# The feed-forward by seven block products for eight, in a fused Conformer and RG-LRU layer on one core

## The chip, the core and the metric

The kernel runs on one core of a Trainium2 chip. A core has five engines that the texts below name: TensorE (PE; PEld is its loading of weights) multiplies matrices, VectorE (DVE) and ScalarE (ACT) work element by element on 128 partitions, GpSimd (POOL) does smaller work of that kind and can start transfers, and SyncE (SP) only starts transfers between the chip's memory and the core's own memory, SBUF. TensorE writes its results into PSUM, from where VectorE or ScalarE must take them. Each engine works through its own instructions in the order of the program and waits at semaphores for the others. The metric is the device time of one execution in microseconds (us).

## What is computed

One inference step of one layer, on 544 tokens (512 of a prompt and 8 x 4 of samples), model width 1024, all in float32. Ahead of the part that matters here come two token mixers, their merge, and a first normalisation; the result is x1. Then:

```
x1  = layer_norm(alpha * x + mix)
hid = square(relu(x1 @ w_ff1))            # w_ff1 1024 x 4096
ff  = hid @ w_ff2                         # w_ff2 4096 x 1024
ple = sigmoid(x1 @ w_ple_gate) * (p @ w_ple_proj)
y   = layer_norm(alpha * x1 + ff + ple)
```

## The kernel before

All activations lie feature by feature: a tile holds 128 channels (partitions) by 544 tokens. float32 products are made in three passes of a shorter format: each operand is split into a high part (`hi`, by ScalarE) and a low part (`lo` = value minus high part, by VectorE), and a product is high x high + high x low + low x high. So each block of 128 x 128 weights against 544 tokens takes three passes, each in two halves of 288 and 256 columns, since a bank of PSUM holds 512.

**Weights** come as chunks of 512 x 256 (128 x 1024 in SBUF, 512 KB), 64 of them for the feed-forward, in the order of use. SyncE loads a chunk into one of `RAW_BUFS = 3` raw buffers, ScalarE makes `hi`, VectorE `lo`, into four buffers each (`SPLIT_BUFS`), and TensorE uses it in `pair`: two column tiles of the output, a PSUM tile `ps` of 1024 columns (two banks; three such buffers, ring `mm`) for each. A second ring `misc` has two PSUM buffers of one bank.

**Feed-forward.** `ff_order` interleaves the four quarters of the first matrix (`evac_ff1`: relu and square by ScalarE from PSUM, then the split) with the four of the second (`evac_ff2`: VectorE adds the PSUM tile to the running sum `acc`). The last quarter is done by token halves (`by_halves`, PSUM tile `psq`), so that the last normalisation (`between3`) starts beside it. The feed-forward has 64 x 48 = 3072 matmuls.

**The order of the program** is written by a planner while the kernel is built. `Clocks` keeps an estimate of when each engine is free and each tile ready. `stream` offers the next load (SP), high part (ACT) or low part (DVE) of the weights, `put` queues sequences of steps beside the products, and `fill`, called after each few matmuls, puts into each engine's queue what its estimated clock allows; `need` forces what is due. What comes out is a fixed order on each engine. Dependencies between engines follow from it: an instruction that writes a tile waits for the earlier readers of that tile, one that reads waits for its writer, by semaphore.

`SLOTS` is the number of activation tiles in SBUF. All instructions of the kernel are recorded by one helper, at line 137 in the program before and line 149 after, so the profile's groups are told apart by the tiles' names.

Of the kernel before, what the change touches and what calls it, by code (L numbers as in the profile page):

```python
# [9 lines left out]
F32 = mybir.dt.float32  # L10
# [5 lines left out]
P = 128  # L16
# [7 lines left out]
# the 544 token columns lie in two PSUM banks, as 256 + 288 neighbouring columns  # L24
# [3 lines left out]
SLOTS = 71  # L28
# [12 lines left out]
LN1_PRIO = 0.1  # L41
STREAM_PRIO = 0.15
# [19 lines left out]

def tname(x):
    return x.tensor.name
# [9 lines left out]
class Clocks:  # L74
    """estimates of when each engine comes to its work, from which the order of issue follows"""
# [35 lines left out]
    def op(self, e, name, out, args, kw):  # L111
# [4 lines left out]
        if e == "D":  # L116
# [25 lines left out]
def tile_hybrid_step(ctx: ExitStack, tc: tile.TileContext, I, O):  # L142
# [35 lines left out]
    # ---------------------------------------------------------------- constants  # L178
# [11 lines left out]
    # TensorE has its full clock only after a stretch of work: begin that while the first loads are under way  # L190
# [5 lines left out]
    # ---------------------------------------------------------------- weight stream  # L196
# [15 lines left out]

    raws, his, splits, held, fast, stacked = {}, {}, {}, set(), set(), set()
# [11 lines left out]
    def parts(j, tag):  # L225
        """a chunk's split weights: one buffer, or two of the activations' for a chunk that is held for long"""
# [34 lines left out]
    def split_first(a, b):  # L261
        """columns a to b of the first chunk, which comes in pieces"""
# [16 lines left out]
    def stream(e, i):  # L279
        """the next load, high or low part of a weight that engine e may take up beside chunk i"""  # L280
# [70 lines left out]
    def fill():  # L351
        horizon = clocks.t["T"] + LEAD
        moved = True
        while moved:
            moved = False
            for e in "DSVGT":
                while clocks.t[e] < horizon:
                    now = clocks.t[e]
                    it = stream(e, state["next"] - 1)
# [23 lines left out]
    # ---------------------------------------------------------------- products  # L383
# [13 lines left out]
    def pair(acts, mt0, evac, nkt=None):  # L397
        """two 128-column tiles of a product; its chunks come next in the stream"""
# [13 lines left out]
    def by_halves(acts, mt0, nmt, evac, between=None):  # L412
        """column tiles, all of the first token half before the second"""
# [21 lines left out]
    def split_later(prio, src, name, done_, due, *deps):  # L435
        """the two parts of an activation as a sequence of its own"""
# [18 lines left out]
    # ---------------------------------------------------------------- stream order  # L455
# [32 lines left out]
    ff_order = [(1, 0), (1, 1), (2, 0), (1, 2), (2, 1), (1, 3), (2, 2), (2, 3)]  # L488
    for kind, q in ff_order:
        if kind == 1:  # L490
            plan(I["w_ff1"][0], D, 1024 * q, 4)
        else:
            for p in range(4):
                for r in range(2):
                    w_spec(I["w_ff2"][0], 1024 * q + 512 * r, 4, 256 * p, 256)
    held.update(range(len(specs) - 4, len(specs)))

    # ---------------------------------------------------------------- x, feature-major
# [27 lines left out]
    # ---------------------------------------------------------------- parameters and states  # L526
# [37 lines left out]
    def param_math():  # L564
        # softplus(-lam) = max(-lam, 0) + 2 atanh(e / (2 + e)), e = exp(-|lam|)
# [19 lines left out]
        # c2 * r is half of -log(a)  # L585
# [3 lines left out]
    # ---------------------------------------------------------------- layer norms  # L589
    class Norm:  # L590
        """mean and variance over the 1024 channels of eight feature-major tiles, per token half"""
# [52 lines left out]
        def put(self, h, prio, due, after, *deps):  # L644
            """queue the steps up to 1 / deviation, and then after()"""
# [101 lines left out]
    # ---------------------------------------------------------------- branch b  # L747
# [519 lines left out]
```

## Time and profile before

| | us |
|---|---|
| median of 3 runs (1005.08 to 1007.27) | 1005.63 |
| span of the profiled execution | 1004.8 |
| around the span, against the median of the runs | 0.8 |
| VectorE busy | 646.2 |
| ScalarE busy | 413.1 |
| GpSimd busy | 179.6 |
| TensorE's unbroken last stretch, nearly all of it feed-forward | 604.57 to 972.31 |

The page gives for each engine busy time, its share of the span and the number of instructions. A group of instructions has the line, engine, operation, the tiles written and read (buffer numbers left out) and their shapes, the count, then busy time and mean nanoseconds, then the idle time before them and what ended most of it. A chain row has start, duration and instruction; a timeline row the same, with the idle time before it and what ended that in brackets. A transfer's row ends with the median time from issue to landing. In a row of the windows stand the stretch, its length, each engine's busy time with its count of instructions, the granted clock of TensorE (1.00 is full), the share in which the DMA engines were busy, and GB/s.

### The profile page before, as it was taken

What the parts mean: (1) busy time and instruction counts of PE and PEld (TensorE: products, weight loads), DVE (VectorE), ACT (ScalarE), POOL (GpSimd) and SP (SyncE); (2) the same over time, 40 slices, a digit from 0 to 9 for tenths busy, and PEclk for the clock granted to TensorE, in tenths of its full rate; (3) what the DMA queues carried; (4) which work ended last, traced back from release to release, by engine and by line L of the source; (5) the groups of instructions that cost most, each with busy time, mean ns of one, the idle gap of its engine ahead of it and who ended that gap; (6) DMA issues with size and microseconds to landing.
All of it is one profiled execution on the core that took longest, in us unless ns stands there. A gap on an engine that the chain in (4) does not pass through costs nothing.

```text
span 1004.8 us, 17739 instructions
## 1 busy us (share of the span) xinstructions
PE 964.2 (96%) x7560; PEld 959.4 (95%) x7560; DVE 646.2 (64%) x939; ACT 413.1 (41%) x600; POOL 179.6 (18%) x173
## 2 busy tenths in 40 slices
PE   8999979989889997999999999999999999999995
PEld 8999979989889997999999999999999999999995
DVE  5698889897899999794468952323322222233447
ACT  6432428643467321563225834455114511541301
POOL 0342765455332700001200000000000000000002
PEclk9999989999899998999999999999999999999998
DMA  8333324332332222326251402222232332222402
GB/s 291 93 95 103 107 65 155 104 100 61 88 117 73 64 78 91 107 84 197 84 169 43 125 24 84 85 84 85 87 99 73 97 108 84 85 84 85 125 29 84
DMA packets 89279, 97.87 MB, mean 97 GB/s; under 512 B 4208, under 2 KB 82416, under 8 KB 89200
## 3 DMA queue, kind: packets, MB, share of 16 engines
q1 hardware_dynamic: 89200, 96.74, 31.1%
q8 instruction: 59, 0.97, 0.4%
q14 instruction: 20, 0.16, 0.1%
HBM read 89.71 MB, written 3.81 MB: 93 GB/s over the span
## 4 chain that ended last, share of the span: by engine, by line
PE 72%; DVE 12%; POOL 7%; ACT 5%; issue 3%; DMA 1%; SPq 0%; DVEq 0%; ACTq 0%; POOLq 0%
PE ps L137 55%; PE psq L137 14%; DVE ca L137 5%; DVE lo L137 2%; POOL prod L137 2%; POOL cbs L137 2%; POOL ctx_b L137 1%; PE pps L137 1%; ACT th L137 1%; PE rg L137 1%; ACT L137 1%; ACT hi L137 1%; ACT aa L137 1%; DVE s L137 1%; DVE th L137 1%
## 5 line engine op out<-in xcount | busy, mean ns | idle before, releaser
L137 ACT ACTIVATE hi<-raw 128x1024 fp32r<-128x1024 f32 (+4 forms) x177 | 167.7, 957 | 284.1 <-PE ps L137 217.2
L137 DVE TENSOR_TENSOR lo<-raw,hi 128x1024 fp32r<-128x1024 f32 (+3 forms) x173 | 194.4, 1148 | 13.2 <-ACT hi L137 13.0
L137 DVE SCALAR_TENSOR_TENSOR ca<-u,par_a,ca 128x482 f32<-128x482 f32 (+29 forms) x240 | 179.6, 806 | 1.3 <-ACT ca L137 0.9
L137 PE MATMUL ps<-x1l,hi 128*128 128x288 f32 x616 | 128.3, 290 | 0.6 <-DVE x1l L137 0.6
L137 PE MATMUL ps<-x1h,hi 128*128 128x288 f32 x616 | 127.6, 289 | 0.6 <-ACT x1h L137 0.6
L137 PE MATMUL ps<-x1h,lo 128*128 128x288 f32 x616 | 127.6, 288 | 0.0
L137 PEld LDWEIGHTS ps<-x1h,hi 128*128 128x128 f32 x616 | 94.8, 189 | 0.8 <-ACT x1h L137 0.8
L137 PEld LDWEIGHTS ps<-x1l,hi 128*128 128x128 f32 x616 | 94.6, 189 | 0.8 <-DVE x1l L137 0.8
L137 PEld LDWEIGHTS ps<-x1h,lo 128*128 128x128 f32 x616 | 94.9, 189 | 0.0
L137 POOL TENSOR_TENSOR y<-y,rows_g 128x512 f32<-128x512 f32 x2 | 3.1, 1547 | 461.1 <-ACT y L137 461.1
L137 DVE TENSOR_TENSOR acc<-acc,ps 128x544 f32<-128x544 f32 x24 | 17.3, 722 | 93.8 <-PE ps L137 93.8
L137 ACT ACTIVATE ff<-ps 128x544 f32<-128x544 f32 x32 | 20.0, 624 | 51.2 <-PE ps L137 51.2
L137 POOL TENSOR_TENSOR prod<-ctx_a,par_a 128x248 f32<-128x248 f32 x32 | 36.9, 1206 | 0.0
L137 PE MATMUL psq<-x1l,hi 128*128 128x288 f32 (+1 forms) x128 | 36.9, 288 | 0.0
L137 PE MATMUL psq<-x1h,lo 128*128 128x288 f32 (+1 forms) x128 | 36.8, 288 | 0.0
L137 PE MATMUL psq<-x1h,hi 128*128 128x288 f32 (+1 forms) x128 | 36.8, 287 | 0.0
L137 PE MATMUL ps<-x0h,hi 128*128 128x288 f32 x104 | 23.2, 306 | 10.5 <-ACT gate L137 9.0
L137 PEld LDWEIGHTS ps<-x0h,hi 128*128 128x128 f32 x104 | 16.7, 198 | 11.7 <-ACT gate L137 9.7
L137 PE MATMUL ps<-x0h,lo 128*128 128x288 f32 x104 | 22.3, 297 | 5.3 <-DVE lo L137 5.3
L137 ACT ACT_TABLE_LOAD x20 | 25.7, 1283 | 1.4 <-PEq L1257 0.7
L137 POOL COPY ctx_b<-bx 128x32 f32<-128x32 f32 x10 | 21.2, 2125 | 26.6 <-ACT bx L137 26.6
L137 POOL TENSOR_TENSOR sa<-sa,sb 128x544 f32<-128x544 f32 x6 | 10.9, 1812 | 77.3 <-DVE sa L137 77.3
(616 smaller groups left out, 2647.7 us busy)
## 6 DMA issues: line engine op xcount, KB each, us to landing
raw<-in_w_ff_dram SPq DMA_DIRECT2D x64, 512.0 KB, 4.2
raw<-in_w_in_dram SPq DMA_DIRECT2D x51, 512.0 KB, 3.6
xr<-in_x_dram SPq DMA_DIRECT2D x16, 272.0 KB, 5.3
raw<-in_w_proj_b_dram SPq DMA_DIRECT2D x8, 512.0 KB, 3.4
raw<-in_w_proj_a_dram SPq DMA_DIRECT2D x8, 512.0 KB, 4.1
raw<-in_w_out_dram SPq DMA_DIRECT2D x8, 512.0 KB, 3.5
raw<-in_w_ple_gate_dram SPq DMA_DIRECT2D x8, 512.0 KB, 3.9
out_dram<-y SPq DMA_DIRECT2D x8, 256.0 KB, 2.0
```

Of the source, the lines that this page charges most:

```text
L137: return fn(out, *args, **kw)
```

## The change

The feed-forward's two products are made by a form of Strassen's and Winograd's scheme for 2 x 2 blocks. With weight blocks A11, A12, A21, A22 (128 x 128 each, several such in a row) and activation blocks B (two channel tiles by two halves of 272 tokens), a product of eight block products becomes seven, from sums of blocks:

| number | weights | activations | goes to PSUM region |
|---|---|---|---|
| 1 | A11 | B11 | al |
| 7 | S3 = A11 + A21 | t3 | de |
| 6 | S2 = S3 + A22 | t2 | al, onto 1 |
| 4 | A22 | t4 | de, onto 7 |
| 5 | S1 = A21 + A22 | t1 | al, onto 1 and 6 |
| 2 | A12 | B21 | be |
| 3 | S4 = S2 + A12 | B22 | al, onto all before |

The table is also the order on TensorE. al and be are the two banks of one PSUM tile of the ring `mm`, de is one of the ring `misc`. After each product its region is read: in the first matrix by ScalarE after 1, 7, 6 and 3 and by VectorE after 4, 5 and 2; in the second always by VectorE, which adds it to a block of `acc` or subtracts it.

The first matrix is done in 16 groups `f0` to `f15` of 256 output channels, the second in five stages `g0` to `g4` over 256-channel blocks of hid, each with four groups of output channels. f0 and g4 stay with plain products (`FOUR`), the others use seven (`SEVEN`): 15 groups of products of 128 x 512 weights (256 KB) and 16 of 128 x 384 (192 KB). The order is f0 to f3, g0, f4 to f6, g1, f7 to f9, g2, f10 to f13, g3, f14, f15, g4.

Of the weight sums, S1 and S3 are made in the transfer: SP loads the first block into a raw buffer, then GpSimd starts an accumulating DMA that adds the second. S2 and S4 are added by VectorE from raw buffers. Two products' weights (units) share a buffer of a ring, of which there are still three raw and four of each split part. Each unit is then split as before. VectorE also makes the activations' forms t1 to t4, which ScalarE and VectorE split. The weights are laid out by blocks in memory. Cut to its core:

```diff
-SLOTS = 71
+SLOTS = 72
+FORM_AHEAD = {"D": 7, "G": 6, "V": 4, "S": 5}
+HALF = T // 2
+SUMS_BY_DMA = True
...
+    SEVEN = ("A11", "S3", "S2", "A22", "S1", "A12", "S4")
+    FOUR = ("A11", "A12", "A21", "A22")
...
+                def load(u=u, first=first, nm=nm):
+                    have_raw(u)
+                    DMA.dma_start(u.raw, u.src[first])
+                    u.full = nm[0] == "A"
+                    u.begun = True
+                task("D", u, lambda u=u: may_have("raw", u.r), lambda: 0.0, load)
+                if nm[0] == "S" and by_dma:
+                    def more(u=u, second=PARTS[nm][1]):
+                        G.dma_start(u.raw, u.src[second], accum_op=OP.add)
+                        u.full = True
+                    task("G", u, lambda u=u: u.raw is not None, lambda: 0.0, more)
...
+        elif by_dma:
+            lo(us["A11"])
+            total(us["S2"], us["S3"], us["A22"])
+            lo(us["S3"]), lo(us["S2"])
+            lo(us["A22"]), lo(us["S1"])
+            total(us["S4"], us["S2"], us["A12"])
+            lo(us["A12"]), lo(us["S4"])
...
+    def seven(fs, name, after):
+        ab, d = mm_psum(name), misc_psum(name + "d")
+        al, be, de = ab[:, :HALF], ab[:, 512:512 + HALF], d[:, :HALF]
+        for nm, ps, start, b in ((1, al, True, "B11"), (7, de, True, "t3"), (6, al, False, "t2"), (4, de, False, "t4"),
+                                 (5, al, False, "t1"), (2, be, True, "B21"), (3, al, False, "B22")):
+            u = take()
+            for k, f in enumerate(fs):
+                mm3(ps, u, k, f()[b], start and k == 0, k == len(fs) - 1, not start)
+                fill()
+            release(u)
+            after(nm, ps)
+            fill()
...
+    def ff2_seven(g):
+        q0, nq = GROUPS[g]
+        for mp in range(4):
+            c = [[half(acc[2 * mp + i], l) for l in range(2)] for i in range(2)]
+            def after(nm, ps):
+                out, op = {1: (c[0][0], V.tensor_add), 7: (c[1][1], V.tensor_sub), 6: (c[1][0], V.tensor_sub),
+                           4: (c[1][0], V.tensor_sub), 5: (c[1][1], V.tensor_sub), 2: (c[0][0], V.tensor_add),
+                           3: (c[0][1], V.tensor_add)}[nm]
+                op(out, out, ps)
+            seven([lambda q=q: hid_forms[q] for q in range(q0, q0 + nq)], f"g{g}_{mp}", after)
```

What this does to the order is seen at three places of the second matrix. On VectorE before, in the second matrix, each pair of readings of PSUM (`acc`) stands between low parts of chunks (`lo`) that are whole loads of SP:

```order
L137 TENSOR_TENSOR acc2_6260<-acc2_6260,ps116_0_7944 128x544
L137 TENSOR_TENSOR acc3_6261<-acc3_6261,ps116_1_7945 128x544
L137 TENSOR_TENSOR lo120_8060<-raw120_7892,hi120_8000 128x1024
L137 TENSOR_TENSOR lo121_8114<-raw121_7950,hi121_8058 128x1024
L137 TENSOR_TENSOR acc4_6262<-acc4_6262,ps118_0_8056 128x544
L137 TENSOR_TENSOR acc5_6263<-acc5_6263,ps118_1_8057 128x544
```

On VectorE now, in the third group of the third stage (`g2_2` is its tile with al and be, `g2_2d` the one with de; `fraw70` holds S1 in its second half, `fraw71` S4 in its second, `fraw72` the next group's A11 and S3, `fraw73` its S2):

```order
L149 TENSOR_TENSOR acc5_6263<-acc5_6263,g2_2_9491 128x272
L149 TENSOR_TENSOR flo70_9509<-fraw70_9449,fhi70_9508 128x384
L149 TENSOR_TENSOR fraw71_9468<-fraw69_9428,fraw71_9468 128x384
L149 TENSOR_TENSOR acc5_6263<-acc5_6263,g2_2d_9492 128x272
L149 TENSOR_TENSOR flo71_9539<-fraw71_9468,fhi71_9538 128x384 x2
L149 TENSOR_TENSOR flo72_9561<-fraw72_9542,fhi72_9560 128x384
L149 TENSOR_TENSOR acc5_6263<-acc5_6263,g2_2_9491 128x272
L149 TENSOR_TENSOR fraw73_9550<-fraw72_9542,fraw73_9550 128x384
L149 TENSOR_TENSOR flo72_9561<-fraw72_9542,fhi72_9560 128x384
L149 TENSOR_TENSOR flo73_9587<-fraw73_9550,fhi73_9586 128x384
L149 TENSOR_TENSOR acc4_6262<-acc4_6262,g2_2_9491 128x272
```

The first row reads product 6, the fourth product 4, the seventh product 5 and the last product 2; the sum S2 of the next group (`fraw73`) now stands between the readings of 5 and 2.

On TensorE in the same group, with the semaphores that an instruction waits for (`hh` and `hl` tiles are high and low parts of activation forms):

```order
L149 MATMUL g2_2_9491<-hh8B_9195,fhi70_9508 128x272
L149 MATMUL g2_2_9491<-hl8B_9228,fhi70_9508 128x272
L149 MATMUL g2_2_9491<-hh8B_9195,flo70_9509 128x272
L149 MATMUL g2_2_9491<-hh6A_8437,fhi71_9538 128x272 [waits DVE_49,Activation_49]
L149 MATMUL g2_2_9491<-hl6A_8470,fhi71_9538 128x272
```

The third row ends product 5, and the fourth begins product 2, in the other bank of the same tile; its wait on VectorE is for the reading of product 5, as the first matmul of product 3 waits for that of product 2.

More of the change, by code (lines that the diff above doesn't have):

```diff
@@ L279, in stream @@
     def stream(e, i):
+        if forms is not None and {"D": state["loaded"], "S": state["hi"], "V": state["lo"]}.get(e, INF) >= len(specs):
+            return forms.offer(e)
         more = 2 if i in fast else 0
@@ L487, in tile_hybrid_step @@
     plan(I["w_ple_gate"][0], D, 0, 4)
[L488 to L496, printed above, removed]
     x = []
@@ new lines, in tile_hybrid_step, with offer, run, take @@
+    add_units.r = add_units.s = 0
+    class forms:
+        @staticmethod
+        def offer(e):
+            if not tasks.get(e):
+                return None
+            i, gate, when, fn = tasks[e][0]
+            if i > at["now"] + FORM_AHEAD[e] or not gate():
+                return None
+            def run():
+                tasks[e].popleft()
+                fn()
+            return when(), run
+    def take():
+        at["now"] += 1
+        u = units[at["now"]]
+        need(NCH + u.i)
+        while not getattr(u, "lo_done", False):
+            moved = False
+            for e in "DGSV":
+                while tasks[e] and tasks[e][0][0] <= u.i + 3 and tasks[e][0][1]():
+                    tasks[e].popleft()[3]()
+                    moved = True
+                    if u.lo_done:
+                        break
+            assert moved, (u.i, u.name, {e: (t[0][0], t[0][1]()) for e, t in tasks.items() if t})
+        fill()
+        return u
```

375 lines of the change are left out of this document (349 added, 26 removed).

## The prediction

> **What bounds the kernel now.** I read the page's busy line first, then the chain of waits, then busy time by stretches.
>
> ```profile
> span 1004.8 us, 17739 instructions
> PE 964.2 (96%) x7560; PEld 959.4 (95%) x7560; DVE 646.2 (64%) x939; ACT 413.1 (41%) x600; POOL 179.6 (18%) x173
> 604.57 336.68 PE ps L137 x2688
> 941.24 31.07 PE psq L137 x240
> 604.57:941.24 336.67, 336.67 (x2690) 336.67 (x2690) 104.23 (x113) 120.24 (x154) 0.00 (x0) 1.00 0.29 88
> ```
>
> TensorE is busy 96% of a span of 1004.8 us; the span is 0.8 below the median of the runs (1005.63); I sum against it and add 0.8. The two chain rows (start, us, what, instructions) say that from 604.57 to 972.31, a stretch that holds nearly all of the feed-forward, TensorE runs without a gap. In the windows row (columns: us; busy us of PE, PEld, DVE, ACT, POOL with counts; clock; DMA share; GB/s) PE is busy 336.67 of 336.67 at clock 1.00, VectorE a third of it, GpSimd not at all, and the DMA engines 0.29. So the stage is bound by matmuls, at 336.68 / 2688 = **0.125 us** each (mean 272 columns, the width of the new ones). Fewer matmuls are worth their full time, as long as nothing makes TensorE wait.
>
> **What the change removes.** Of the 3072 feed-forward matmuls, 324 go: a group of eight block products becomes one of seven, 15 times in the first matrix (a product has 12 matmuls of 272 columns) and 16 times in the second (9 matmuls), 15 x 12 + 16 x 9. 324 x 0.12525 = **40.6 us**. What stays plain (block f0, 96 matmuls, and group g4, 384) costs 12.0 + 48.1. A product takes 1.50 us in the first matrix and 1.13 in the second, seven of them 10.5 and 7.9.
>
> **What it adds: waits inside each group.** The prices of a handover come from these rows.
>
> ```profile
> 941.28 0.72 DVE L137 TENSOR_TENSOR acc<-acc,ps 128x544 f32<-128x544 f32 x1 [2.29 <-PE ps L137]
> 941.92 2.35 DVE L137 TENSOR_TENSOR lo<-raw,hi 128x1024 fp32r<-128x1024 f32 x2
> 944.46 0.46 DVE L137 TENSOR_TENSOR acc<-acc,psq 128x288 f32<-128x288 f32 x1 [0.19 <-PE psq L137]
> 969.51 0.42 DVE L137 TENSOR_TENSOR acc<-acc,psq 128x256 f32<-128x256 f32 x1 [2.39 <-PE psq L137]
> 349.66 1.94 DVE L137 TENSOR_TENSOR lo<-raw,hi 128x1024 fp32r<-128x1024 f32 x1
> 351.65 0.52 PE L137 MATMUL ps<-x0h,lo 128*128 128x288 f32 x2 [0.88 <-DVE lo L137]
> 352.01 0.42 PE L137 MATMUL ps<-x1h,hi 128*128 128x288 f32 x2
> 352.26 0.42 PE L137 MATMUL ps<-x1l,hi 128*128 128x288 f32 x2
> 948.00 2.49 DVE L137 TENSOR_TENSOR lo<-raw,hi 128x512 fp32r<-128x512 f32 x4
> L137 DVE TENSOR_TENSOR lo<-raw,hi 128x512 fp32r<-128x512 f32 x32 | 20.4, 685 | 1.4 <-ACT hi L137 1.3
> 949.22 1.16 ACT L137 ACTIVATE hi<-raw 128x512 fp32r<-128x512 f32 x2 [1.44 <-DMA raw<-in_w_ff_dram]
> ```
>
> In the new order of products (1, 7, 6, 4, 5, 2, 3) the first matmul of product 2 carries a wait for VectorE's reading of product 5, and that of product 3 for its reading of product 2: the two halves al and be lie in different banks, but in one PSUM tile, and the program orders by tile. Both waits fall with no product between, so they are on the path. One costs: the pair of matmuls listed with 0.42 while pairs follow every 0.25 (352.01 to 352.26) drains 0.16; VectorE reads 272 columns in 0.44 (between 0.42 and 0.46); TensorE starts 0.05 after a VectorE end (351.60 to 351.65); its first pair takes 0.36 instead of 0.25 (351.65 to 352.01), 0.11; VectorE starts 0.04 after a TensorE end (604.57 + 336.68 = 941.25, then 941.28). Sum **0.80 us** with VectorE free. Twice in 31 groups: 31 x 1.6 = 49.6 us, already more than the 40.6 saved. This holds with an idle VectorE; behind other work each is longer.
>
> Between the two waits stands VectorE's queue. It works in the order of the program, and beside the evacuations it has two weight sums and seven low parts a group: start to start 0.60 us for 512 columns (four in 2.49, of which the last has 0.685: 1.80 / 3) and some 1.14 for 1024 (two in 2.35, the last about 1.2), so by the straight line 0.47 for 384 and 0.35 for 272. Two high parts of ScalarE take 1.16, one after the other every 0.53 if the last has about 0.63.
>
> **What it adds: a serial chain through two DMAs.** Raw weights still have three buffers. So the first half of the next group's S3 can only be loaded when VectorE has finished S4's sum, or S1's low part, of this group; then GpSimd adds the second half; then VectorE sums S2 from it. In 15 of the 31 groups (I call them B: every other one) the order on VectorE has that S2 sum *ahead of* the reading of product 2. All behind it waits: the reading, and so product 3, and the low parts that the next group needs. In the other 16 (N) the reading comes first.
>
> ```profile
> raw<-in_w_rg_dram SPq DMA_DIRECT2D x4, 192.0 KB, 2.4
> raw<-in_w_proj_b_dram SPq DMA_DIRECT2D x4, 256.0 KB, 2.9
> q1 hardware_dynamic: 89200, 96.74, 31.1%
> ```
>
> A plain load lands 2.4 us after issue for 192 KB (second matrix) and 2.9 for 256 KB (first). No transfer of GpSimd is in this trace, nor an accumulating one. Let T be its time to landing: it reads what it writes, so from below I bound it by the plain load (2.4 / 2.9), a gain below that being excluded as it moves the same bytes and more, and from above by two such loads in a row (4.8 / 5.8). I take T = 3.0 and 3.3, near the plain row, since the queue's engines are busy only 31.1%. The Trainium skill, "DMA: Bandwidth & Descriptors", section "Anatomy of one DMA — SWDGE (gpsimd) path", fits 2.0 us + bytes / 436e3 per transfer on GpSimd's path, an estimate of 2.45 and 2.60 here; by it the sum below would be some 9 us lower. No row of before shows such a transfer.
>
> A B group of the second matrix, from the start of product 7: products 7 and 6 end at 2.25; drain and start 0.20; reading of product 6 0.35, low part of S1 0.47 (3.27), S4 sum 0.47 (3.74). The load starts after one or the other, 3.5 on the mean, lands at 5.9, the accumulation at 5.9 + T. Then S2's sum and two low parts 3 x 0.47 = 1.41; the reading of product 2 and the restart 0.60; product 3 and the next product 1, 2.25. In all 10.2 + T = **13.2** against 7.9 of matmuls.
> B in the first matrix: ScalarE reads product 1 (0.35) and makes three high parts (1.6), low part of S1 0.60 (2.55), load 2.9 (5.4), T, S2's sum 0.60, an activation's low part of 544 columns 0.64, a low part 0.60, reading and restart 0.60, products 3 and 1 3.0: 10.9 + T, **14.2**.
> An N group has the two waits, 0.8 and, with part of a low part ahead of product 5's reading, about 1.0, and in the second matrix some 1.0 in which the next S3's low part is late (two low parts of 0.47 behind the sum): 7.9 + 2.8 = **10.7**; in the first 10.5 + 1.8 = **12.3**. Here T is hidden up to about 3.4.
>
> Sum: 8 x 13.2 + 8 x 10.7 + 7 x 14.2 + 8 x 12.3 = 389 us, plus 60.1 plain, 449; before 3072 x 0.12525 = 384.8. **+64 us.**
>
> **The clock.** Each B group stops TensorE for 2 us and more, once or twice. In the trace:
>
> ```profile
> 143.60 0.49 PE L137 MATMUL rg<-span,hi 96*128 96x288 f32 x2 [2.19 <-issue]
> 145.70:152.40 6.70, 5.47 (x22) 5.15 (x23) 6.64 (x10) 0.87 (x2) 3.65 (x5) 0.50 0.17 49
> 217.78 0.82 PE L137 MATMUL ps<-x0h,hi 128*128 128x288 f32 x2 [2.92 <-ACT gate L137]
> 217.40:220.70 3.30, 2.92 (x13) 2.92 (x14) 3.30 (x6) 1.79 (x3) 0.80 (x2) 0.50 0.10 34
> 287.91 0.51 PE L137 MATMUL ps<-x0h,lo 128*128 128x288 f32 x2 [3.08 <-DVE lo L137]
> 289.10:292.40 3.30, 3.30 (x16) 3.30 (x16) 3.30 (x6) 0.78 (x1) 0.00 (x0) 0.50 0.92 276
> 381.60 0.52 PE L137 MATMUL ps<-hb0h,lo 128*128 128x288 f32 x2 [1.47 <-DVE lo L137]
> 381.70:387.90 6.20, 2.67 (x20) 2.46 (x20) 6.20 (x10) 1.06 (x1) 0.00 (x0) 1.00 0.26 85
> 388.58 0.82 PE L137 MATMUL ps<-hb0h,hi 128*128 128x288 f32 x2 [4.21 <-DVE sb L137]
> 388.00:394.80 6.80, 6.21 (x27) 6.22 (x28) 6.80 (x11) 0.82 (x1) 0.00 (x0) 0.50 0.49 157
> ```
>
> Gaps of 2.19, 2.92, 3.08 and 4.21 us are each followed by a stretch at clock 0.50; one of 1.47 is not. A stretch loses its busy time less 0.125 per matmul: 5.47 - 2.75 = 2.7, 2.92 - 1.63 = 1.3, 3.30 - 2.00 = 1.3, 6.21 - 3.38 = 2.8. I take 1.3 for each of the 15 B groups, the lower end, since part of the slowed work lies before a wait that ends when it would anyway: **+20 us**; the ends are 0 and 15 x 2.8 = 42. The Trainium skill, "TensorE: Matmul & The Clock Gate", section "HAM oscillation — how this bites in real kernels", has it that only idle gaps over about 3.4 us cost the clock; by that the 20 us would mostly vanish. The rows of 2.19 to 3.08 speak against it here.
>
> Forecast: 1004.8 + 64 + 20 + 0.8 = **1090 us**, 85 above before.
>
> **What is hidden.** SP loads 40.6 MB in place of 33.6 for the feed-forward (five units of a group instead of four blocks), GpSimd 14.2 MB (two units); that fits in DMA engines that are busy 0.29 of this stage, and GpSimd has 0.00 to do there. VectorE's own work is about 10.2 of 10.5 us in a first-matrix group (7 x 0.60, 2 x 0.60, three readings, four forms and four low parts of activations) and 6.7 of 7.9 in the second; ScalarE's 9.2 of 10.5. At the group times above all this has room; if the waits were gone, VectorE would be the next limit in the first matrix, within 4% of TensorE. More activation forms are made there ahead of their use; if that cover went, one 544-column low part (0.64) a block, 10 us in all, would be late.
>
> **Rivals.**
> *Matmuls stay the limit* (faster): the waits on the PSUM tile end before TensorE comes, and each S3 is there in time. 1005.6 - 40.6 = **965**. For it: TensorE was never late in this stage. Against: product 2 follows product 5 directly, so a reading of 0.44 cannot be over before. It decides only if a handover costs below 0.65 us (40.6 / 62), against 0.80.
> *Only the handovers* (slower): the loads start early enough to hide T; +49.6 - 40.6 = +9, with the late low parts and the longer of the two waits (31 x 0.2 + 16 x 1.0) +31: **1015 to 1037**. Against: a raw buffer holds two units, three of them less than a group, and the next S3 takes one that this group still reads.
> *The chain, clock kept, T plain*: 64 - 8 = +56, 1062; if the B groups also lost less against N than 2.5 and 1.9 us (8 x 2.5 + 7 x 1.9 = 33, say 25 of it hidden) it falls to 1037; with some clock loss, 8 more: **1037 to 1070**. For it: the gap of 1.47 that kept its clock. Against: every B group has a longer one by the sums above. The Trainium skill's rule on gaps, above, would lead here.
> *Accumulation slow*: T at its upper ends adds 8 x 1.8 + 7 x 2.5 = 32; with 42 of clock loss instead of 20, 1090 + 54: **1110 to 1144**. In N groups T would show as well.
> That the change doesn't do what it says can be excluded for the matmuls, which are counted; the sums by DMA are 62 in GpSimd's queue.
>
> **How the numbers follow.** Forecast (1070 to 1110) 0.40; clock kept 0.20; slow accumulation 0.22; only handovers 0.13; matmul-bound 0.05. A measurement here can tell about 0.2%, 2 us. Faster 0.05, same 0.02 (the low edge of the handovers), slower 0.93. The range leaves out the matmul-bound case, the lower half of the handovers and the top of the slow accumulation: **1020 to 1140**.
>
> **What would show it.** In the new trace: product 2's and 3's first matmuls with idle time before them named to VectorE's acc or form operations, at least 0.7 us each; VectorE idle on a GpSimd DMA of raw weights in every second group, and TensorE gaps of 2 to 4 us there; PEclk digits below 9 in the feed-forward slices; T in the DMA issues, against 3.0 and 3.3. Wrong if TensorE's share there stays above 95%, if the gaps are alike in all groups, or if the sums' landing is hidden and the time is below 1030.

## The result and the profile after

The changed kernel takes **1169.45 us** (median of 4 runs, 1169.15 to 1170.63) against 1005.43 in runs beside it: 1.164 times as long, 95% interval 1.162 to 1.166. Slower was forecast, but 1090 us, and the range ended at 1140. The first lines of the page, the share of TensorE's clock over the span in tenths, and the rows of the feed-forward's transfers (the last number is the time from issue to landing; SPq is SyncE's queue, POOLq GpSimd's):

```profile
span 1167.9 us, 18411 instructions
PE 988.7 (85%) x7236; PEld 963.0 (82%) x7236; DVE 824.2 (71%) x1399; ACT 494.5 (42%) x875; POOL 227.2 (19%) x235
PEclk9999989989999999999999887988888889978898
fraw<-in_w_ff_dram SPq DMA_DIRECT2D x95, 256.0 KB, 3.3
fraw<-in_w_ff_dram SPq DMA_DIRECT2D x80, 192.0 KB, 2.9
fraw<-in_w_ff_dram POOLq DMA_DIRECT2D x30, 256.0 KB, 4.6
fraw<-in_w_ff_dram POOLq DMA_DIRECT2D x32, 192.0 KB, 3.8
```

324 matmuls are gone, and yet TensorE is busy longer (988.7 us for 964.2) and idle for 15% of the span instead of 4%. Up to the feed-forward little changed: it begins at 604.40 us before and 603.30 now. Nearly all of the difference lies in the 31 groups of seven, which run from 615.95 to 1102.28: 486.3 us, where eight products took 324.6 (2592 matmuls of 0.12525). Windows of one B group (`g2_2`), of the N group behind it, and of the whole stretch of the 31 groups, in the columns of before:

```profile
906.50:923.71 17.21, 10.71 (x66) 10.00 (x65) 9.24 (x20) 5.85 (x12) 1.73 (x2) 0.76 0.45 107
923.71:934.64 10.93, 9.25 (x64) 8.87 (x64) 5.36 (x12) 1.05 (x2) 1.05 (x2) 0.91 0.31 103
616.00:1102.00 486.00, 347.77 (x2267) 328.04 (x2267) 271.14 (x546) 191.21 (x406) 51.80 (x60) 0.86 0.43 102
```

The two groups have the same 63 matmuls (7.9 us at full clock); one takes 17.2 us, the other 10.9. The clock column says that TensorE ran at half speed in part of the first. The last row says the same of the whole: 348 us of matmuls for 284 at full pace, and 138 us without any. From the starts of TensorE's instructions in the trace, mean time from product 1 to the next group's product 1:

```
                   matmuls  forecast   measured
B, first matrix     10.5      14.2      21.2   (7 groups, 19.6 to 23.3)
B, second           7.9       13.2      17.6   (8 groups, 15.8 to 20.0)
N, first            10.5      12.3      13.6   (8)
N, second           7.9       10.7      11.0   (8)
sum of the 31      284.1     389       486.3
```

So the pattern was as forecast, group by group, and the B groups were mis-sized. The chain of waits through the B group `g2_2` shows where its time is (start, duration, what):

```profile
911.12 0.04 DVE acc L149
911.15 0.32 issue
911.47 0.56 DVE flo L149
912.03 0.02 issue
912.05 0.33 SPq L149
912.38 0.05 issue
912.43 2.91 DMA fraw<-in_w_ff_dram
915.34 0.02 issue
915.37 0.04 POOLq L149
915.41 0.48 issue
915.89 0.01 POOLq L149
915.90 3.32 DMA fraw<-in_w_ff_dram
919.22 0.02 issue
919.25 0.57 DVE fraw L149
```

VectorE reads product 6 (911.12), makes S1's low part (911.47), and with that a raw buffer is free; SP starts the load of the next A11 (912.05) and of S3's first half (912.43), which takes 2.91 us; 0.6 us later GpSimd's accumulating transfer starts and lands after 3.32; then VectorE sums S2 (919.25). What TensorE does meanwhile, in the timeline:

```profile
912.06 0.29 PE L149 MATMUL g<-hh6B,fhi 128*128 128x272 f32 x1
916.15 0.56 PE L149 MATMUL g<-hh6A,fhi 128*128 128x272 f32 x1 [2.81 <-DVE acc L149]
916.51 0.43 PE L149 MATMUL g<-hl6A,fhi 128*128 128x272 f32 x1
916.74 0.43 PE L149 MATMUL g<-hh6A,flo 128*128 128x272 f32 x1
921.53 0.57 PE L149 MATMUL g<-hh6B,fhi 128*128 128x272 f32 x1 [3.00 <-ACT fhi L149]
```

Product 5 starts at 912.06, product 2 after 2.81 idle us and product 3 after 3.00 more, both at half clock: their matmuls follow every 0.23 us (916.51 to 916.74), not every 0.125. The trace names ScalarE at the second wait, as the last signal near it; by the program both waits are for VectorE's readings, and the one of product 2 stands behind the sum at 919.25 in VectorE's queue (920.95). The first wait hangs on the same release of the raw buffer. In VectorE's queue the reading of product 5 stands behind the low part of the next A11, which waited for that block's load and high part:

```profile
915.10 0.56 DVE L149 TENSOR_TENSOR flo<-fraw,fhi 128x384 fp32r<-128x384 f32 x1 [1.32 <-ACT fhi L149]
915.58 0.43 DVE L149 TENSOR_TENSOR acc<-acc,g 128x272 f32<-128x272 f32 x1
```

### The profile page after: what moved, and what is told of

The parts are those of the page before. It is cut to its first block, busy times and chain, and to the rows that moved or that the text cites. A ratio compares the mean times of both kernels' runs of the same rounds, so it can differ in the third digit from the quotient of the medians.

```text
span 1167.9 us, 18411 instructions
## 1 busy us (share of the span) xinstructions
PE 988.7 (85%) x7236; PEld 963.0 (82%) x7236; DVE 824.2 (71%) x1399; ACT 494.5 (42%) x875; POOL 227.2 (19%) x235
## 4 chain that ended last, share of the span: by engine, by line
PE 41%; DVE 23%; DMA 15%; ACT 8%; POOL 7%; issue 5%; SPq 1%; POOLq 0%; ACTq 0%; DVEq 0%
DMA fraw<-in_w_ff_dram 14%; PE ps L149 14%; PE psq L149 12%; DVE ca L149 8%; PE f L149 6%; PE g L149 5%; DVE lo L149 3%; DVE flo L149 3%; ACT fhi L149 2%; POOL prod L149 2%; DVE fraw L149 2%; POOL cbs L149 1%; POOL ctx_b L149 1%; ACT fy L149 1%; PE pps L149 1%
## 5 line engine op out<-in xcount | busy, mean ns | idle before, releaser
L149 ACT ACTIVATE fhi<-fraw 128x512 fp32r<-128x512 f32 (+1 forms) x229 | 123.8, 572 | 243.9 <-DMA fraw<-in_w_ff_dram 170.1
L149 DVE TENSOR_TENSOR flo<-fraw,fhi 128x512 fp32r<-128x512 f32 (+1 forms) x229 | 137.8, 621 | 28.1 <-ACT fhi L149 26.6
L149 POOL DMA_DIRECT2D fraw<-in_w_ff_dram x62 | 53.7, 866 | 497.6 <-DMA fraw<-in_w_ff_dram 230.8
L149 ACT ACTIVATE hi<-raw 128x1024 fp32r<-128x1024 f32 (+3 forms) x109 | 100.0, 928 | 111.7 <-PE ps L149 62.0
L149 DVE TENSOR_TENSOR lo<-raw,hi 128x1024 fp32r<-128x1024 f32 (+3 forms) x105 | 121.0, 1165 | 11.2 <-ACT hi L149 11.0
L149 PE MATMUL f<-x1h,fhi 128*128 128x272 f32 x212 | 68.2, 334 | 60.6 <-DVE fy L149 43.3
L149 PE MATMUL f<-x1h,flo 128*128 128x272 f32 x212 | 64.8, 318 | 0.2 <-DVE flo L149 0.2
L149 PE MATMUL f<-x1l,fhi 128*128 128x272 f32 x212 | 64.9, 318 | 0.0
L149 PEld LDWEIGHTS f<-x1h,flo 128*128 128x128 f32 x212 | 45.5, 220 | 0.5 <-DVE flo L149 0.5
L149 PEld LDWEIGHTS f<-x1l,fhi 128*128 128x128 f32 x212 | 45.7, 220 | 0.0
L149 POOL TENSOR_TENSOR sa<-sa,sb 128x544 f32<-128x544 f32 x6 | 10.9, 1814 | 76.9 <-DVE sa L149 76.9
```

The lines of the kernel that those rows point to most:

```text
L149: return fn(out, *args, **kw)
```

## The experiments

All were run beside the kernel before, whose median was 1005.2 to 1006.9 us in them. Gains below are against 1169.45. The times of groups and gaps are worked out as in the table above. The planner writes the order anew for most edits, so more moves than the line that is shown: in the first four, by the tiles' names in the traces, between a fifth and a half of VectorE's feed-forward instructions stand elsewhere. With the filled waits and with the plain transfers the order is the changed kernel's on every engine.

### Four single edits

**The next S2 sum behind the reading of product 2** (a planner limit that lets VectorE's weight work run four units ahead):

```diff
-FORM_AHEAD = {"D": 7, "G": 6, "V": 4, "S": 5}
+FORM_AHEAD = {"D": 7, "G": 6, "V": 3, "S": 5}
```

> Only the place of the next group's S2 sum on VectorE changes: behind the reading of product 2 instead of ahead of it. Chain theory: in the B groups of the changed kernel (16.6 to 23 us from one product 7 to the next) products 3 and 1' lie behind the landing of the accumulating transfer; moved, they run while it lands, and product 7' starts about 0.7 us after the landing. That takes 1.8 + 2.2 + 1.9 - 0.7 = 5.2 us off each of 8 B groups of the second matrix and 2.4 + 2.9 + 2.2 - 0.8 = 6.7 off each of 7 of the first: 1169 - 88 = about 1080 us (1065 to 1110). Rival, PSUM handovers set the time: under 10 us gained, since both waits of the tile stay. Rival, transfers or the clock alone set it: under 25 gained, the waits only move from product 3 to product 7'.

Measured: 1122.4 us (1120.2 to 1124.0), 47 us gained. B groups fell from 21.2 to 15.8 and from 17.6 to 14.9, but N groups grew from 13.6 to 14.3 and from 11.0 to 11.7. In none of the groups does the sum stand ahead of that reading now. So the reordering was worth 47 us of the 88 expected; the next group's S3 load was still issued 4.8 and 4.3 us after product 7's start in B groups (4.7 and 5.1 without the edit), and later than before in N groups.

**Region be in a tile of its own:**

```diff
-        ab, d = mm_psum(name), misc_psum(name + "d")
-        al, be, de = ab[:, :HALF], ab[:, 512:512 + HALF], d[:, :HALF]
+        ab, d, e = mm_psum(name), misc_psum(name + "d"), misc_psum(name + "e")
+        al, be, de = ab[:, :HALF], e[:, :HALF], d[:, :HALF]
```

> Region be gets a PSUM tile of its own (of the ring of one-bank tiles), so that product 2 doesn't wait for the reading of product 5, nor product 3 for that of product 2; the planner then also puts the next S2 sum behind the reading of product 2. Chain theory: the gain of the later sum (88 us) and the two handovers of the 16 N groups besides, 1.2 to 1.6 us each, 19 to 26: 1169 - 110 = about 1060 us (1045 to 1085), and the gaps before products 2 and 3 fall under 0.2 us in N groups. Rival, handovers alone: 31 x 1.6 = 50 gained, 1119. Rival, transfers or clock: as N groups only, 1145.

Measured: 1127.9 us (1125.6 to 1129.7), 41.5 gained, no more than by the first edit, which it contains in 11 of the 15 B groups. The gaps before product 2 went from 44 us to 0 and those before product 3 from 79 to 15, as expected; but 59 us of gaps before product 7 are new (7 before). In its list of waits (us in all, times, longest) product 7's tiles of the second matrix have appeared, and wait for the next S3:

```profile
PE g_1d L149 <- ACT fhi L149: 10.0, 4, 3.1
PE g_3d L149 <- ACT fhi L149: 7.1, 4, 2.8
PE g_0d L149 <- ACT fhi L149: 6.9, 4, 2.6
```

Now B and N groups take nearly alike, as long as one passage from buffer to product 7: on the mean 15.0 us in the first matrix (B 15.9, N 14.2) and 13.3 in the second. The handovers cost nothing as long as this chain is longer. The forecast of 88 and 110 us was wrong in taking the N groups' slack as given; they had it because B groups were so long.

**Four raw buffers:**

```diff
-SLOTS = 72
-RAW_BUFS = 3
+SLOTS = 70
+RAW_BUFS = 4
```

> Four raw buffers for three (two activation tiles fewer), order otherwise by the same planner. Chain theory: the load of the next S3 no longer waits for this group's sum S4 or low part of S1 (4.7 and 5.1 us after product 7's start in B groups), so the chain starts some 4 us earlier in 15 groups: 1169 - 60 = about 1110 us (1095 to 1130). Rival, PSUM handovers: no change (under 5 us). Rival, transfers slow because of their load on the queues: under 20 gained, since the same bytes move.

Measured: 1061.3 us (1060.2 to 1064.2), 108 gained, nearly twice what was expected. The difference of B and N groups is gone (13.5 and 13.8; 10.7 and 10.7), no product 7 waits, and the clock is 0.97. The load of the next S3 is issued some 3.5 to 9 us *before* product 7 of the group, and GpSimd's result lies ready 1 to 7 us before VectorE takes it up for S2 (longer before the very first group). Its windows row, for the 31 groups:

```profile
620.00:996.80 376.80, 313.69 (x2271) 298.82 (x2271) 268.50 (x546) 189.70 (x406) 51.88 (x60) 0.97 0.54 132
```

What is left is 58 us of gaps before products 2 and 3. There one handover can be read with nothing else in it (timeline, product 2 of `g2_2` in this kernel):

```profile
862.07 0.36 PE L149 MATMUL g<-hh6A,fhi 128*128 128x272 f32 x1 [0.62 <-DVE acc L149]
```

0.62 us idle, and 0.29 of the matmul before it where 0.125 is the pace: 0.79 later than without a wait, and the product itself takes 0.08 longer than its like, 0.87 in all for 0.80 in the prediction.

**Without the second summand of S1 and S3**, so without any of GpSimd's 62 transfers:

```diff
-                        G.dma_start(u.raw, u.src[second], accum_op=OP.add)
                         u.full = True
```

> Leaves out the second summand of S1 and S3 (no transfers by GpSimd at all); everything else stays. Chain theory: lag and landing go, 0.6 + 3.7 us in 8 B groups, 0.7 + 4.5 in 7: 1169 - 71 = about 1100 us (1085 to 1120), with gaps of 1 to 3 us left before products 2 and 3 in B groups. Rival, PSUM handovers: no change. Rival, contention of the accumulating transfers with SP's loads: more than 90 gained, SP's landing back from 2.9 and 3.3 to 2.4 and 2.9.

Measured: 1063.6 us (1061.8 to 1064.9), 106 gained: 21 us below the range of the theory, and more than the 90 that the rival of contention asked for. SP's landings:

```profile
fraw<-in_w_ff_dram SPq DMA_DIRECT2D x95, 256.0 KB, 2.9
fraw<-in_w_ff_dram SPq DMA_DIRECT2D x80, 192.0 KB, 2.8
```

They were 3.3 and 2.9 us beside the accumulating transfers. The 256 KB loads fell as that rival had it, the 192 KB loads only by 0.1, where it had 0.5; over 15 B groups that is some 4 us. The rest of the surplus goes with the release: the next S3 is now loaded 0.1 and 0.5 us *before* product 7, not 4.7 and 5.1 after. That an earlier landing lets VectorE free the next buffer earlier, so that the gain feeds itself, is argued from the order, not tried. Taking the second transfer out of the chain and starting the chain earlier end at the same place, and for the same reason: both bring the chain below the handovers, with 55 and 58 us of gaps left before products 2 and 3.

### The size of two terms

**The clock.** Matmuls of no use fill part of TensorE's waits in the B groups:

```diff
+WARM = {(2, "f"): 6, (3, "f"): 32, (2, "g"): 10, (3, "g"): 20}
+LATE = "f2 f4 f6 f8 f10 f12 f14 g0_0 g0_2 g1_1 g1_3 g2_0 g2_2 g3_0 g3_2".split()
...
             u = take()
+            for i in range(WARM.get((nm, name[0]), 0) if name in LATE else 0):
+                nc.tensor.matmul(de, ones, fs[0]()["B11"][0], start=True, stop=True)
```

> The changed kernel with work added: in the 15 B groups TensorE makes 6 or 10 matmuls of no use ahead of product 2 and 32 or 20 ahead of product 3 (first or second matrix; into region de, which has been read by then), 0.8 to 4 us that fit into its waits there. Nothing else moves. Theory, the clock is a large term (the matmuls of the 31 groups took 348 us of busy time for 284 at full clock): products 3, 1' and 7' run at full clock behind the waits, 1.8 us in 8 groups and 2.1 in 7, and some of products 7' and 6' besides: 1169 - 30 to 50 = 1119 to 1140 us. Rival, the slowed products lie before a wait that ends anyway: under 10 gained. Rival, the added matmuls lengthen the waits: slower by up to 15 x 3 = 45 us.

Measured: 1153.3 us (1149.6 to 1155.0), 16 gained, between the theory and its rival. The windows row of the 31 groups shows the clock at 0.97 for 0.86:

```profile
617.38:1087.47 470.09, 387.55 (x2776) 366.32 (x2775) 270.85 (x546) 190.79 (x406) 51.78 (x60) 0.97 0.45 106
```

In the changed kernel the matmuls' busy time is 64 us above full pace: 15 of it is the listed end of the last matmul before each wait (0.29 us for a pace of 0.125), and 48 are matmuls that followed each other more slowly than every 0.19 us. With the filling the groups' own matmuls keep 21 of the 48. So 27 us of slow pace went for 16 us of time; where the other 11 went is not shown.

**The adding.** The same transfers, without adding:

```diff
-                        G.dma_start(u.raw, u.src[second], accum_op=OP.add)
+                        G.dma_start(u.raw, u.src[second])
```

> The changed kernel with GpSimd's 62 transfers plain instead of accumulating, so that they overwrite the first summand of S1 and S3, which is left out; order and waits are the same on every engine. Theory, the adding costs: landing falls from 3.8 and 4.6 us to about SP's 2.9 and 3.3, 15 x 1.1 = 17 us off, about 1152 (1145 to 1160). Rival, it is the way of GpSimd's queue (0.87 us of its own time for each) that costs: landing stays, 1164 to 1172.

Measured: 1149.75 us (1147.9 to 1151.2), 20 gained; the kernel's transfer rows:

```profile
fraw<-in_w_ff_dram POOLq DMA_DIRECT2D x30, 256.0 KB, 3.2
fraw<-in_w_ff_dram POOLq DMA_DIRECT2D x32, 192.0 KB, 3.1
fraw<-in_w_ff_dram SPq DMA_DIRECT2D x95, 256.0 KB, 3.1
fraw<-in_w_ff_dram SPq DMA_DIRECT2D x80, 192.0 KB, 2.9
```

Adding costs 0.7 us for 192 KB and 1.4 for 256 KB. Without it GpSimd's queue lands as fast as SP's, within 0.2 us.

### Combinations

**The tile and four raw buffers** (both diffs above):

> Both edits that were tried singly: region be in a PSUM tile of its own, and four raw buffers. With four buffers alone the gaps before products 2 and 3 sum to 58 us in the 31 groups and the rest of the groups' time beyond their matmuls to 30. Theory, raw buffers bound and handovers hidden behind them: with the bound moved, the handovers are worth their time, 1061 - 58 = about 1003 us; the chain of load, lag, landing and high part (3.4 + 0.6 + 3.9 + 0.5 = 8.4 us) is then longer than a second-matrix group's 7.9, so some wait before product 7 comes back: 990 to 1025. Rival, the handovers cost nothing in either case (as the tile alone suggests: 1127.9 with it, 1122.4 with the later sum alone): 1045 or more.

Measured: 1026.9 us (1025.4 to 1029.3). The tile that was worth nothing beside the first edit is worth 34 us here: the handovers were hidden behind the chain. The time is 2 us above the range; 33 us of gaps are left, 15 of them before products 6 and 4 (groups of 12.0 and 9.9 us).

**VectorE sums instead of transfers**, alone and with both edits:

```diff
-SUMS_BY_DMA = True
+SUMS_BY_DMA = False
```

> The changed kernel with only S1 and S3 summed by VectorE in place of the accumulating transfers; three raw buffers and one PSUM tile for al and be as they were. Theory, the serial chain through two transfers: like the kernel without second parts (1063.6), plus two VectorE sums a group where VectorE is late: 1065 to 1090 us. Rival, three buffers are too few whatever fills them: over 1120, since units still wait for a buffer. Rival, VectorE is the limit: 15 x 0.9 us above 1063 in the first matrix only.

Measured alone: 1073.6 us (1069.3 to 1076.0), as the theory of the two transfers had it. Three buffers as such were not the limit. Nor did VectorE hold the first matrix only, as the last rival had it: against the kernel without the second summand, groups of both matrices grew alike, by 0.4 us. The setting does more than the expectation says: SP then loads four blocks of a group instead of five (144 loads for 175), as S3 is summed from blocks that are there already.

> As the kernel with the tile and four raw buffers, and S1 and S3 summed by VectorE instead of accumulating transfers. VectorE's own work is then 11.4 us of a first-matrix group of 10.5 and 7.6 of 7.9. Theory, VectorE becomes the limit in the first matrix and the landing disappears in the second: 15 x 11.6 + 16 x 8.6 + 113 us for the rest of the feed-forward, about 1000 us (985 to 1020). Rival, the accumulating transfers are free once there are four buffers: then VectorE's extra sums make it slower than with tile and buffers alone, by 10 to 20 us.

Measured with tile and four buffers: 1011.1 us (1007.8 to 1015.4), 16 faster than with transfers; its ratio to before is 1.005 (1.003 to 1.007). So the accumulating transfers, with the fifth load that goes with them, are not free even with a fourth buffer, and VectorE's 62 sums cost less than they.

**Seven in the second matrix only**, with transfers and with VectorE's sums:

```diff
-        add_units(SEVEN if n else FOUR, "w_ff1", n, 0, 4)
+        add_units(FOUR, "w_ff1", n, 0, 4)
...
-        (ff1_seven if n else ff1_four)(n)
+        ff1_four(n)
```

> As the kernel with the tile and four raw buffers, but the first matrix with eight plain products (12.0 us a group, as before); seven only in the second, by accumulating transfers. It removes 144 matmuls, 18 us. Theory, the chain of 8.4 us limits second-matrix groups to 9 to 9.5 us: 16 x 9.3 = 149 for 144.3 before, so 1005 + 5 = 1010 us (1000 to 1020). If the chain is hidden by the fourth buffer: 16 x 8.1, 990. Rival, VectorE was what made the first matrix slow: then this one gains more over tile and buffers than the 15 x 0.7 us that plain products cost there.

> Seven products in the second matrix only, all four sums by VectorE, region be in a tile of its own, five raw buffers (four activation tiles fewer). In the kernel with VectorE's sums and four buffers such groups ran in 8.1 to 8.8 us once a stage was under way, and took 10 to 13 for the first of a stage, against 9.0 for eight products. Theory, only late forms and weights at a stage's start are left, and the plain first matrix gives them room: 16 x 8.3 = 133 for 144.3, 1006 - 11 = 995 us (988 to 1003). Rival, the start of a stage stays late: 4 x 3.5 us more, 1009 (1004 to 1014).

Measured: 1030.1 us (1027.6 to 1032.7) and 1011.6 (1010.3 to 1012.9). The first missed its theory's range by 10 us; of the second the rival came true. A second-matrix group took 10.1 us with transfers, not 9.3, and 9.0 with VectorE's sums, just what eight products take; the first two groups of most stages took 10.0 beside 8.2.

**Activation forms ranked behind the weights** in the planner, on top of VectorE's sums (one number):

```diff
-        put(0.1, steps, due)
+        put(0.3, steps, due)
```

> As the kernel with seven products in the second matrix only and all sums by VectorE, but four raw buffers (two activation tiles more), and the activation forms of a block rank behind the weights' parts in the planner. There the first two groups of a stage took 10.0 us for 8.2 and the feed-forward began 4 us later than with 70 activation tiles. Theory, the forms of the block just finished, not needed until the next stage, stood ahead of the weights on VectorE: 4 + 6 x 1.7 = 14 us off 1011.6, about 998 (994 to 1003), faster than before. Rival, only the 4 us of the activation tiles come back: 1006 to 1009.

> As the kernel with own tile, four raw buffers and VectorE's sums in both matrices (1011.1), with the activation forms ranked behind the weights' parts. Six groups there (f1, f3, g0.1, g1.0, g2.0, f13) took 23 us more than their like. Theory, half of it goes: about 1000 us (992 to 1006). Rival, VectorE is full in the first matrix (11.4 us of work a group), the forms only come later elsewhere: 1008 to 1016.

Measured: 1010.2 us (1007.3 to 1011.1) and **1007.1** (1005.5 to 1009.8), short of both theories: the first is 1 us above its rival's range, the second lies between its theory's (to 1006) and its rival's (from 1008). The second, seven products in both matrices, is the same as before: ratio 1.001 (0.9996 to 1.0024). Its first-matrix groups reach 10.5 to 11.0 us (all but the first), the price of their matmuls, but the second matrix's groups go from 9.3 to 9.9, the first of a stage taking 12.2 to 13.1. That the forms, now later, are what holds them is argued, not tried. Of its 31 groups:

```profile
619.88:940.30 320.42, 297.88 (x2270) 288.43 (x2269) 296.02 (x608) 191.04 (x406) 0.00 (x0) 0.99 0.30 91
```

VectorE (third busy column) is as busy as TensorE, 296 of 320 us. Eight products took 324.6 for the same groups, with VectorE busy a third of the time.

**Transfers in the first matrix, VectorE in the second**, without and with that ranking:

```diff
-        by_dma = SUMS_BY_DMA
+        by_dma = w == "w_ff1"
```

> Own tile, four raw buffers; S1 and S3 by accumulating transfers in the first matrix only (30 transfers), by VectorE in the second. VectorE's work is then 10.2 of 10.5 us a first-matrix group and 7.6 of 7.9 in the second, 60.9 of 63.1 us of matmuls in three groups of the first and four of the second; with all sums by VectorE it was 64.5. Theory, VectorE's total was what held the two all-VectorE kernels at 1007 to 1011: with 3.6 us less for each of five such stages, 18 us off 1011: about 993 us (986 to 1002), faster than before. Rival, the chain of 8.4 us through two transfers and the late forms hold first-matrix groups at 12.0 us as in the kernel with accumulating sums throughout: 15 x 12.0 + 16 x 9.0, 1010 to 1018.

> The same with the activation forms ranked behind the weights' parts. Theory as there, and first-matrix groups at 10.6 us as in the all-VectorE kernel with forms behind: 985 to 998. Rival, forms and weights only trade places between the stages as they did there (1011 to 1007): within 5 us of the kernel without the ranking.

Measured: 1027.3 us (1025.7 to 1029.8) and 1021.1 (1017.0 to 1024.8). The first lies 9 us above even its rival's range: first-matrix groups took 12.7 and 11.9 us with transfers, 11.7 and 10.9 with VectorE's sums. The second gained 6 us by the ranking, far from its theory. No version ran faster than before.

### The start of the chain

**Product 7 read later by ScalarE:**

```diff
             elif nm == 7:
-                S.activation(half(b["X"], 1), ps, AF.Copy)
+                b["d"] = ps
             elif nm == 6:
+                S.activation(half(b["X"], 1), b["d"], AF.Copy)
```

> The changed kernel with one move: in the first matrix ScalarE reads product 7 after product 6 instead of right after product 7, so that S1's high part stands ahead of that reading in ScalarE's queue, not behind it. Theory, the load of the next S3 came late there (5.1 us after product 7's start instead of the 2.55 of the prediction) since S1's high part stood behind a wait for product 7's end: the release falls to 3 to 3.5 us in the 7 B groups, 7 x 1.8 = 13 us off; product 4 then waits for the reading, 0.7 us in the 8 N groups, 6 on: about 1162 us (1156 to 1166). Rival, other work of ScalarE and VectorE (the forms of the block before) sets the release: it stays above 4.5 us and the time rises to 1172 to 1180.

Measured: 1168.4 us (1164.0 to 1170.5), no change that can be told. The release fell in three of the seven B groups of the first matrix (f4, f10, f14: 4.6, 4.6, 5.4 to 3.1, 3.1, 3.4 us) and stayed in the others (f2, f6, f12 at 5.6 to 6.0, f8 at 3.7). B groups of the first matrix went from 21.2 to 20.0 us, all other groups grew by 0.1 to 0.3. Those three follow the second matrix; the other four follow a first-matrix block, whose relu, squares and forms stand in the queues of ScalarE and VectorE. That these hold the release there is read off the timeline, not tried.

## Why the prediction was wrong in size

**What bounds it, and what goes.** Right. 324 fewer matmuls, and with all waits gone 31 groups would take 284.1 us of the 324.6 of before.

**The handover.** Right in mechanism and nearly in price (0.80 forecast, 0.87 read), but not additive. The 49.6 us that were set against the saving count all 62 of them; beside a longer chain they were worth nothing (the tile alone), without it 34 us. In N groups both waits were there, 0.5 to 1.8 us idle each.

**The chain through two transfers.** Right in its place: 15 B groups, with the order on VectorE that was quoted. Both ways of breaking it gave back 106 to 108 of the 164 us. This is the step whose terms were mis-sized. From product 7 to the next group's product 7, in B groups (1' is the next group's product 1):

```
                                   second matrix        first matrix
                                 forecast measured    forecast measured
next S3's load issued after        3.5      4.7         2.55     5.1
load to landing                    2.4      3.2         2.9      3.3
GpSimd starts after the landing    -        0.6         -        0.7
accumulation, issue to landing     3.0      3.7         3.3      4.5
sum to product 3                   2.0      1.8         2.4      2.4
products 3 and 1'                  2.25     4.1         3.0      5.1
in all                            13.2     18.1        14.2     21.1
```

The differences over 8 and 7 groups are 27 us for the issue, 9 for the load, 10 for GpSimd's start, which the sum lacked altogether, 14 for the accumulation, and 29 for products 3 and 1' at half clock, less 2 between the landing and product 3. The forecast had 20 of this under the clock, which leaves 67; some 10 in the N groups, counted in the same way, and 2 outside the groups make the 79 us of the error. That the clock is what lengthened products 3 and 1' is shown by the filled waits: there they took 2.5 and 3.4 us. In the forecast's words: "ScalarE reads product 1 (0.35) and makes three high parts (1.6)" left out what stood ahead of S1's high part in ScalarE's order: the reading of product 7, which delayed the release in three groups of seven, and, read off the timeline but not tried, the activations of the block before in the others; "the load starts after one or the other, 3.5 on the mean" left out that products 7 and 6 were slowed and late themselves (3.2 us on the mean from the start of 7 to the end of 6, for 2.25); and T was taken "near the plain row" where no row of such a transfer existed. The upper bound of two plain loads in a row, 4.8 and 5.8, held it; but the upper end of the range was made from that bound and the clock alone, while the terms that failed most had been given no bounds.

**The clock.** +20 us forecast; 16 were gained by keeping TensorE busy, which removed 27 of the 48 us of slow pace. TensorE's gaps before product 3 of the B groups were 2.6 to 5.9 us, where 2 to 4 were forecast. The rule that was weighed, the Trainium skill's "TensorE: Matmul & The Clock Gate", section "HAM oscillation — how this bites in real kernels", that there should be no idle gaps over some 3.4 us, was read as if shorter ones cost nothing. That reading fails here: product 2 of `g2_2` ran at half pace (0.23 us a matmul) behind a gap of 2.81. The measurement decides.

**The Trainium skill's fit for GpSimd's transfers** ("DMA: Bandwidth & Descriptors", section "Anatomy of one DMA — SWDGE (gpsimd) path"), 2.45 and 2.60 us as estimates, was too low in both forms: 3.1 and 3.2 plain, 3.8 and 4.6 adding.

**The rivals.** That matmuls would stay the limit, or only the handovers cost, is excluded by the changed kernel's own trace, in which B groups take 17.6 and 21.2 us. "Accumulation slow" gave 1110 to 1144 and was the nearest; its mechanism was there, but it holds 14 of the 79 us.

**What stays open.** Why the fastest kernel of seven products keeps 22 us of gaps in its groups; what the planner's reordering, and not the edit itself, added to the gains of the first four edits; whether a better order on VectorE would leave seven products ahead. VectorE's 296 us of 320 say that little room is left there.

## What to carry to other kernels

Fewer matmuls pay only where the work that replaces them (sums, low parts, readings of PSUM) has its own slack: here 40.6 us were saved on TensorE and in the fastest version with seven products VectorE's share of the stage went from a third to nine tenths. A ring of buffers that holds less than one group ties each group's first load to the last group's last sum; count that loop through every queue that it passes, in order, and only then the waits beside it. Two waits in parallel do not add: the tile was worth 0 beside the chain and 34 us without it.

## What the runs showed of the hardware

An accumulating transfer from GpSimd took 0.7 (192 KB) and 1.4 us (256 KB) longer to land than the same transfer without adding, and a plain one from GpSimd as long as one from SP (3.1 and 3.2 against 2.9 and 3.1). GpSimd was busy 0.87 us for each that adds and 0.54 for a plain one, and began 0.6 us after the landing that it waited for. The plain loads of 192 and 256 KB landed in 2.9 and 3.3 us in this kernel, in 2.8 and 2.9 without GpSimd's transfers, and in 2.4 and 2.9 in the kernel before for other weights of these sizes. Behind gaps of 2.81 and 3.00 us matmuls of 272 columns followed each other every 0.23 us, not every 0.125.
